# Feed-forward products of a hybrid decoder step on 2x2 blocks, with seven multiplications in place of eight

## Chip, cores and metric

The kernel runs on one core of one Trainium2 chip. The time is device microseconds of one execution, given as the median of several; a profiled execution has a time of its own, and its trace covers the span from the first to the last instruction. The engines are TensorE (PE, with its weight loads as PEld), VectorE (DVE), ScalarE (ACT), GpSimd (POOL) and SyncE (SP), which issues nearly all DMAs.

## What is computed

One layer of a decoder over 1024 prompt rows and 8 sample rows (1032 columns here, as tokens lie along the free dimension), all float32: a mixer (chunked gating and an RWKV-7 recurrence), cross-attention, a feed-forward part, and a final norm.

```python
def sq_relu_ffn(h, w_up, w_down):
    return jnp.square(jax.nn.relu(h @ w_up)) @ w_down
...
        x = x + y_mix
        x = x + cross_attn(rmsnorm(x, norm_x_g[l]), mem_k, mem_v, w_xq[l], w_xo[l])
        x = x + sq_relu_ffn(rmsnorm(x, norm_ffn_g[l]), w_up[l], w_down[l])
...
    y_prompt = rmsnorm(xp, final_g)
```

w_up is 1024 x 4096, w_down 4096 x 1024.

## The kernel before

Products keep float32 accuracy by splitting each operand into a high part that the PE takes (fp32r) and a low part, the rest. `gemm` (L132) runs three products for each 128 rows of the sum: high x high, high x low, low x high. `split` makes the parts: ACT casts (L99), DVE or POOL subtracts (L100).

Phase 1 is the mixer, in a hand-written order (`ORDER`). Phase 2 goes on in SBUF: the output projection w_out (`residual` splits each new row block of x into `x2`), the attention by heads, the projection w_xo (L1089, L1090: x is put together again from its two parts and added to), and `ffn`. A scheduler places the instructions of each engine by a model of their times, so program order and engine order differ a little; engines take their own instructions in order.

`ffn` goes through 8 groups of 512 hidden rows. For each of 4 tiles of 128 hidden rows it loads w_up columns (POOL scales them by the norm's weights, L115; ACT and DVE split), runs 3 blocks of 260, 260 and 512 tokens with 24 products each, and turns the result into the split square of its positive part (ACT L1281, L1282; POOL L1283; DVE L1284). Then the group's part of w_down: 8 tiles of 128 output rows, 3 blocks each, 12 products, added to `acc` by DVE (L1295). The hidden rows never leave SBUF. In the last group the blocks are finished in turn, and `last_norm` normalises and stores a tile while the next block's products run:

```python
            for (b0, b1), tiles in zip((*self.BLOCKS[0:2], (520, 776), (776, 1032)), ((0, 1), (2, 3, 8), (4, 5), (6, 7))):
                for m in range(KT):
                    down(ws[m], m, b0, b1)
                self.last_norm(tiles[0:2], acc, r2, gfin, f1, f2, pf)
```

Of the kernel before, what the change touches and what calls it, by code (L numbers as in the profile page):

```python
# [68 lines left out]
class K:  # L69
    ORDER = order()  # L70

    def __init__(self, ctx, tc, a, o, phases=9, dbg=None):
# [952 lines left out]
    def phase2(self, phases):  # L1025
        nc, tc, a = self.nc, self.tc, self.a
        N0 = HALF + NB

        def pool(cx, name, bufs, **k):
            return cx.enter_context(tc.tile_pool(name=name, bufs=bufs, reuse_waits="tile", **k))  # L1030
        with ExitStack() as c2:

            self.o0, self.x0, x1 = (pool(c2, nm, 1) for nm in ("o0", "x0", "x1"))
# [4 lines left out]
            self.ssacc = self.x0.tile([P, T], F32, name="ssacc")  # L1038
            self.x2 = [half(self.x0, "x20", 0), half(x1, "x21", 1)]
            with ExitStack() as c3:  # L1040
                o1 = pool(c3, "o1", 1)
                o = [half(self.o0, "o0", 0), half(o1, "o1", 1)]
                with ExitStack() as c4:
                    self.t2 = pool(c4, "t2", 2)
                    t2b = pool(c4, "t2b", 4)
                    for i, (h0, h1) in enumerate(((0, N0), (N0, T))):
                        oh, ol = o[i]
                        for k in range(0, KT, 2):
                            st = (t2b if i else self.t2).tile([P, 2, HALF], F32, tag="ost", name="ost")
                            nc.sync.dma_start(st, self.d_o[i][k:k + 2].rearrange("k p t -> p k t"))  # L1050
                            self.split(oh[:, k:k + 2, 0:HALF], ol[:, k:k + 2, 0:HALF], st)
                        if i == 0:
                            st = self.t2.tile([P, KT, NB], F32, tag="oss", name="oss", bufs=1)
                            nc.sync.dma_start(st, self.d_os.rearrange("k p t -> p k t"))
                            self.split(oh[:, :, HALF:], ol[:, :, HALF:], st)
                    for i, blocks in enumerate((((0, N0 // 2), (N0 // 2, N0)), ((N0, T),))):
                        for m in range(KT):
                            w = self.load_w(a["w_out"][0][:, m * P:(m + 1) * P])
                            n = N0 if i == 0 else HALF
                            xt = self.t2.tile([P, N0], F32, tag="xnew", name="xn")[:, 0:n]  # L1060
                            nc.sync.dma_start(xt, self.d_x[m][:, i * N0:i * N0 + n])
                            for b0, b1 in blocks:
                                ps = self.pg.tile([P, 512], F32, tag="g", name="ps_g")[:, 0:b1 - b0]
                                self.gemm(ps, w, *o[i], slice(b0 - i * N0, b1 - i * N0))
                                x = xt[:, b0 - i * N0:b1 - i * N0]
                                nc.vector.tensor_tensor(x, ps, x, op=ALU.add)  # L1066
                                self.residual(m, x, b0, b1, m == 0)
                self.ah = [half(self.o0, "o0", 0), half(o1, "o1", 1)]
                with ExitStack() as c4:
                    self.q1, self.q2 = pool(c4, "q1", 1), pool(c4, "q2", 2)  # L1070
                    self.pa = pool(c4, "pa", 2, space=PSUM)
                    self.sp = self.q1.tile([P, 2, NB, NB], F32, name="sp8")
                    nc.gpsimd.memset(self.sp, 0.0)
                    self.token_rs((0, 1, 2, 3, 8))
                    self.token_rs((4, 5, 6, 7))
                    for h in range(4):
                        self.attention(h, (1, 0, 2, 3))
                        if phases == 2:
                            return
                self.t2 = pool(c3, "t3", 2)  # L1080
                blocks = ((0, N0 // 2), (N0, T), (N0 // 2, N0))
                for ms in ((0, 1), (2,), (3,), (4,), (5,), (6,), (7,)):
                    ws = {m: self.load_w(a["w_xo"][0][:, m * P:(m + 1) * P]) for m in ms}
                    for m, (b0, b1) in [(m, b) for b in blocks for m in ms]:
                        ps = self.pg.tile([P, 512], F32, tag="g", name="ps_g")[:, 0:b1 - b0]
                        xh, xl, cols = self.halves(b0, b1)
                        self.gemm(ps, ws[m], *self.ah[0 if b0 < N0 else 1], cols)
                        x = self.t2.tile([P, N0], F32, tag="xnew", name="xn")[:, 0:b1 - b0]
                        nc.vector.tensor_tensor(x, ps, xh[:, m, cols].bitcast(F32), op=ALU.add)  # L1089
                        nc.vector.tensor_tensor(x, x, xl[:, m, cols].bitcast(F32), op=ALU.add)  # L1090
                        self.residual(m, x, b0, b1, m == 0)
            with ExitStack() as c5:
                self.ffn(pool(c5, "f1", 1), pool(c5, "f2", 2), pool(c5, "pf", 4, space=PSUM))
# [280 lines left out]
```

## Time and profile before

| | us |
|---|---|
| median of 3 runs | 1862.61 (1858.98 to 1871.34) |
| profiled execution, its time | 1867.79 |
| its span | 1866.1 |
| first feed-forward product | 1115.51 |
| last feed-forward product | 1854.90 |

Times in the views count from the start of the span. A row of the timeline gives start, length, engine, line, operation, output <- inputs, the tile's partitions x elements and how often; in brackets stands how long the engine had been idle and what ended that.

### The profile page before, as it was taken

What the parts mean: (1) busy time and instruction counts of PE and PEld (TensorE: products, weight loads), DVE (VectorE), ACT (ScalarE), POOL (GpSimd) and SP (SyncE); (2) the same over time, 40 slices, a digit from 0 to 9 for tenths busy, and PEclk for the clock granted to TensorE, in tenths of its full rate; (3) what the DMA queues carried; (4) which work ended last, traced back from release to release, by engine and by line L of the source; (5) the groups of instructions that cost most, each with busy time, mean ns of one, the idle gap of its engine ahead of it and who ended that gap; (6) DMA issues with size and microseconds to landing.
All of it is one profiled execution on the core that took longest, in us unless ns stands there. A gap on an engine that the chain in (4) does not pass through costs nothing.

```text
span 1866.1 us, 33959 instructions
## 1 busy us (share of the span) xinstructions
PE 1735.4 (93%) x13965; PEld 1545.9 (83%) x13965; DVE 1026.5 (55%) x2123; ACT 631.3 (34%) x1253; POOL 625.8 (34%) x530
## 2 busy tenths in 40 slices
PE   6998887998995699999999999999999999999998
PEld 6887777887884588878887898999998999999997
DVE  5697787679758846656565566324232323232335
ACT  4545443554432244433333332131312121212133
POOL 6551332134238563664333343121212121111210
PEclk8999887999896899999999999999999999999999
DMA  4413312111213483545443111112121202020212
GB/s 134 114 46 98 119 57 81 55 57 58 68 47 87 138 246 108 166 148 168 148 147 103 35 46 40 51 40 62 34 62 32 68 23 68 24 68 29 64 44 92
DMA packets 235884, 152.84 MB, mean 82 GB/s; under 512 B 20616, under 2 KB 219680, under 8 KB 235728
## 3 DMA queue, kind: packets, MB, share of 16 engines
q1 hardware_dynamic: 235684, 150.65, 27.1%
q8 instruction: 110, 1.80, 0.4%
q14 instruction: 46, 0.38, 0.1%
q10 hardware_dynamic: 44, 0.01, 0.0%
HBM read 131.07 MB, written 19.56 MB: 81 GB/s over the span
## 4 chain that ended last, share of the span: by engine, by line
PE 73%; DVE 13%; DMA 4%; issue 4%; ACT 3%; POOL 2%; SPq 0%; DVEq 0%; POOLq 0%; ACTq 0%
PE ps_g L132 59%; PE ps_kv L132 2%; PE ps_so L1232 2%; PE psgram L494 1%; DMA qb<-d_q 1%; DVE ptmp L555 1%; PE ps_o L1169 1%; PE psx L630 1%; POOL ck L1212 1%; DVE pb L556 1%; DVE st L466 1%; PE ps_sc L1155 1%; PE psz L638 1%; DVE sp L1187 1%; PE psf L616 1%
## 5 line engine op out<-in xcount | busy, mean ns | idle before, releaser
L132 PE MATMUL ps_g<-x,wh 128*128 128x260 f32 (+3 forms) x2048 | 445.3, 312 | 1.6 <-ACT rl L1281 1.6
L132 PEld LDWEIGHTS ps_g<-x,wh 128*128 128x128 f32 x2048 | 334.6, 189 | 28.0 <-ACT rl L1281 2.9
L132 PE MATMUL ps_g<-x,wl 128*128 128x260 f32 (+3 forms) x1024 | 317.2, 311 | 0.0
L132 PE MATMUL ps_g<-xh,wh 128*128 128x256 f32 (+1 forms) x704 | 217.6, 309 | 11.8 <-DVE raw L365 6.8
L99 ACT CAST wh<-wst 128x1024 fp32r<-128x1024 f32 x124 | 129.8, 1048 | 288.0 <-PE ps_g L132 208.9
L132 PE MATMUL ps_g<-xl,wh 128*128 128x256 f32 (+1 forms) x704 | 213.5, 303 | 1.1 <-DVE xl L100 1.1
L132 PE MATMUL ps_g<-xh,wl 128*128 128x256 f32 (+1 forms) x704 | 211.6, 301 | 0.1
L132 PE MATMUL ps_g<-sl,wdh 128*128 128x260 f32 (+1 forms) x672 | 211.5, 320 | 0.0
L132 PE MATMUL ps_g<-sh,wdh 128*128 128x260 f32 (+1 forms) x672 | 211.4, 320 | 0.0
L1295 DVE TENSOR_TENSOR acc<-ps_g,acc 128x260 f32<-128x260 f32 (+1 forms) x200 | 98.8, 500 | 198.9 <-PE ps_g L132 198.9
L100 POOL TENSOR_TENSOR wl<-wst,wh 128x1024 fp32r<-128x1024 f32 x70 | 171.0, 2443 | 107.8 <-ACT wh L99 92.1
L132 PE MATMUL ps_g<-sh,wdl 128*128 128x260 f32 (+1 forms) x672 | 204.5, 320 | 0.0
L132 PEld LDWEIGHTS ps_g<-x,wl 128*128 128x128 f32 x1024 | 192.6, 189 | 11.8
L115 POOL TENSOR_TENSOR wst<-wst,prm 128x1024 f32<-128x1024 f32 x40 | 76.0, 1901 | 329.6 <-DVE wdl L100 163.9
L132 PE MATMUL ps_g<-o,wh 128*128 128x260 f32 (+1 forms) x768 | 177.1, 325 | 3.1 <-DVE xn L1066 1.9
L1283 POOL TENSOR_TENSOR rl<-rl 128x260 f32<-128x260 f32 (+1 forms) x96 | 76.2, 795 | 247.6 <-ACT sh L1282 247.5
L132 PEld LDWEIGHTS ps_g<-xh,wh 128*128 128x128 f32 x704 | 143.6, 204 | 18.1 <-DVE raw L365 7.3
L132 PEld LDWEIGHTS ps_g<-xl,wh 128*128 128x128 f32 x704 | 143.3, 204 | 6.6 <-issue 2.4
L132 PEld LDWEIGHTS ps_g<-xh,wl 128*128 128x128 f32 x704 | 143.1, 203 | 3.8 <-issue 1.4
L132 PEld LDWEIGHTS ps_g<-o,wh 128*128 128x128 f32 x768 | 128.9, 191 | 16.5 <-issue 3.2
L1284 DVE TENSOR_TENSOR sl<-rl,sh 128x260 fp32r<-128x260 f32 (+1 forms) x96 | 50.1, 525 | 154.3 <-POOL rl L1283 154.3
L132 PEld LDWEIGHTS ps_g<-sh,wdh 128*128 128x128 f32 x672 | 126.0, 188 | 10.2
(444 smaller groups left out, 3392.1 us busy)
## 6 DMA issues: line engine op xcount, KB each, us to landing
wst<-in_w_in_dram SPq DMA_DIRECT2D x44, 512.0 KB
wst<-in_w_up_dram SPq DMA_DIRECT2D x32, 512.0 KB
wdst<-in_w_down_dram SPq DMA_DIRECT2D x64, 256.0 KB
wst<-in_w_out_dram SPq DMA_DIRECT2D x16, 512.0 KB
ck<-in_cache_mem_k_dram SPq DMA_DIRECT2D x32, 256.0 KB
ck<-in_cache_mem_v_dram SPq DMA_DIRECT2D x32, 256.0 KB
sbv<-d_sv SPq DMA_DIRECT2D x40, 128.0 KB
xt<-in_x_prompt_dram SPq DMA_DIRECT2D x8, 512.0 KB
```

The source lines that it names most:

```text
L99: (heng or nc.scalar.copy)(hi, src)
L100: (eng or nc.vector).tensor_tensor(lo, src, hi.bitcast(F32), op=ALU.subtract)
L115: nc.gpsimd.tensor_tensor(st, st, g.unsqueeze(2).broadcast_to([P, KT, P]), op=ALU.mult)
L132: nc.tensor.matmul(ps, l[:, k, :], r[:, cols], start=(k == 0 and i == 0), stop=(k == kt - 1 and i == 2))
L466: nc.vector.scalar_tensor_tensor(st[hr, :, h, 0:64], cs3(kkn[hr, :]), -1.0, lam[hr, :, 0:C], op0=ALU.mult, op1=ALU.mult)
L494: nc.tensor.matmul(psgs[h][:, ci, :], bk[hr, c].rearrange("p j t -> p (j t)"), st[hr, c, h, :], start=True, stop=True)
L555: nc.vector.tensor_tensor(tv, blocks[:, :, t + 1:16, t:t + 1].broadcast_to(shape), blocks[:, :, t:t + 1, 0:t].broadcast_to(shape), op=ALU. ...
L556: nc.vector.tensor_tensor(dst, dst, tv, op=ALU.add)
L1232: nc.tensor.matmul(po, pt[:, t, b, :], vts[b // 2][:, b % 2, t, :], start=(n == 0), stop=(n == 15))
L1283: nc.gpsimd.tensor_tensor(r[:, 0:n], r[:, 0:n], r[:, 0:n], op=ALU.mult)
L1284: nc.vector.tensor_tensor(sl[:, 0, b0:b1], r[:, 0:n], sh[:, 0, b0:b1].bitcast(F32), op=ALU.subtract)
L1295: nc.vector.tensor_tensor(acc[:, m, b0:b1], ps, acc[:, m, b0:b1], op=ALU.add)
```

## The change

Both feed-forward products are done on 2x2 blocks with Winograd's form of Strassen's scheme: seven block products of combined operands, and sums of the results. The token axis is cut in two halves of 516 columns (`HT`), which are one side of the blocks, and pairs of 128-row tiles are the other. An operand in `self.b` holds the seven combinations of 256 rows of x or of hidden rows, in high and low parts; there are four of them at a time (`cb0`, `cb1`, and two in the tiles that held the attention output). 16 turns (`turn`) make 256 hidden rows each, 16 more add 1024 hidden rows to 256 output rows. A turn is 7 steps (`STEPS`) of 2 half-blocks (258 columns, `HS`) of 12 products.

Per turn the weights of the next one are loaded in two tiles of 512 KB and combined on POOL (L1153 of the new file, 4 times), their 7 combinations split by ACT and DVE (L102, L103). Results are added up in `up` or `down`: PSUM to SBUF by ACT (2 steps) or DVE (5 steps), SBUF sums by POOL and DVE. Finished hidden rows go to DRAM (`d_h`), 256 rows or 1.06 MB per turn; each down turn but the last loads such a pair into the one buffer `hr` and replaces an operand with its combinations (L1118 on POOL, 4 times; ACT and DVE split 7). The last up turn replaces all four operands. x is written to DRAM after w_out and after w_xo (`d_x`), and kept as one float32 tile (`yq`) in place of two parts. The final norm starts when all products are done. Two pools of phase 1 change places.

```diff
@@
-        self.sb, self.xp, self.sa, self.s1 = (c1.enter_context(tc.tile_pool(name=nm, bufs=1)) for nm in ("sb", "xp", "sa", "s1"))
+        self.sb, self.sa, self.xp, self.s1 = (c1.enter_context(tc.tile_pool(name=nm, bufs=1)) for nm in ("sb", "sa", "xp", "s1"))
@@
...
+                        nc.sync.dma_start(self.d_x[m][:, i * N0:i * N0 + n], xt)
...
+            c3.close()
+            cb, yq, self.wx, hr = (pool(c2, nm, n) for nm, n in (("cb", 1), ("yq", 1), ("wx", 2), ("hr", 1)))
+            self.ssacc = yq.tile([P, T], F32, name="ssx")
+            self.yq = [yq.tile([P, 2, T], F32, name=f"yq{i}") for i in range(4)]
+            self.hr = hr.tile([P, 2, T], F32, name="hr")
+            self.b = [self.operand(cb, f"cb{i}") for i in range(2)]
+            with ExitStack() as c4:
+                self.t2 = pool(c4, "t3", 2)
+                self.cross_out()
+            self.b += [self.operand(self.o0, "o0"), self.operand(o1, "o1")]
+            f1 = pool(c2, "f1", 1)
+            pq, pf = pool(c2, "pq", 2, space=PSUM), pool(c2, "pf", 2, space=PSUM)
+            self.ffn(f1, pq, pf)
+
+    STEPS = (("A11", 0), ("S1", 3), ("S2", 4), ("S4", 2), ("S3", 5), ("A12", 1), ("A22", 6))
+    def operand(self, pl, tag):
+        t = pl.tile([P, 2, 7, HT], F32R, tag=tag, name=f"c_{tag}")
+        return t[:, 0], t[:, 1]
+    def combine(self, b, x, *what):
+        nc = self.nc
+        b11, b12, b21, b22 = (x[:, j, h * HT:(h + 1) * HT] for j in range(2) for h in range(2))
+        for c in what:
+            if isinstance(c, str):
+                dst, p, q = {"T1": (b11, b12, b11), "T3": (b12, b22, b12), "T2": (b22, b22, b11), "T4": (b21, b21, b22)}[c]
+                nc.gpsimd.tensor_tensor(dst, p, q, op=ALU.subtract)
+                continue
+            src = {0: b11, 1: b21, 2: b22, 3: b11, 4: b22, 5: b12, 6: b21}[c]
+            self.split(b[0][:, c], b[1][:, c], src)
+    AHEAD = {0: (0, "T1"), 1: (3, "T3"), 3: (2, "T2", 4), 4: (5,), 5: (1, "T4"), 6: (6,)}
+    def features(self, i):
+        nc, x = self.nc, self.yq[i]
+        for j in range(2):
+            nc.vector.tensor_scalar(x[:, j], x[:, j], self.g["norm_ffn_g"][:, 2 * i + j:2 * i + j + 1], None, op0=ALU.mult)
+        self.combine(self.b[i], x, *(c for n in range(7) for c in self.AHEAD.get(n, ())))
+    def hidden(self, step, b, pair, x):
+        if step == 0:
+            self.nc.sync.dma_start(x, self.d_h[pair])
+        self.combine(b, x, *self.AHEAD.get(step, ()))
+    def weights(self, step, it):
+        nc = self.nc
+        W, R = self.w.setdefault(it, ({}, {}))
+        def split(n):
+            k = 7 * it + [x[0] for x in self.STEPS].index(n)
+            pl, tag = ((self.wp, "wh"), (self.wp, "wl"), (self.wx, "wx"))[k % 3]
+            t = pl.tile([P, 2, 4, P], F32R, tag=tag, name=f"w{n}")
+            W[n] = t[:, 0], t[:, 1]
+            self.split(t[:, 0], t[:, 1], R[n])
+        def comb(n, dst, x, y, op):
+            R[n] = R[dst] if dst else self.wx.tile([P, 4, P], F32, tag=n, name=f"r{n}", bufs=1)
+            nc.gpsimd.tensor_tensor(R[n], R[x], R[y], op=op)
+        if step == 0:
+            if it < 16:
+                rows, cols, src = (0, 4), it, self.a["w_up"][0]
+            else:
+                rows, cols, src = (it - 16, it - 12), it % 4, self.a["w_down"][0]
+            src = src.rearrange("(i k p) m -> p i k m", k=2, p=P)[:, :, :, cols * 256:(cols + 1) * 256]
+            for r in range(2):
+                t = self.wp.tile([P, 4, 256], F32, tag="wst", name=f"wr{r}")
+                for q0, q1 in ((rows[0], min(rows[1], 16)), (16, rows[1])):
+                    if q0 < q1:
+                        nc.sync.dma_start(t[:, q0 - rows[0]:q1 - rows[0]], src[:, q0 % 16:q0 % 16 + q1 - q0, r])
+                R[f"A1{r + 1}"], R[f"A2{r + 1}"] = t[:, :, 0:P], t[:, :, P:256]
+        elif step == 1:
+            comb("S3", None, "A11", "A21", ALU.subtract)
+            comb("S1", "A21", "A21", "A22", ALU.add)
+            comb("S2", None, "A22", "S3", ALU.subtract)
+        elif step == 2:
+            split("A11")
+        elif step == 3:
+            split("S1")
+        elif step == 4:
+            split("S2")
+            comb("S4", "S2", "A12", "S2", ALU.subtract)
+        elif step == 5:
+            split("S4")
+        elif step == 6:
+            split("S3")
+            split("A12")
+            split("A22")
+    def turn(self, it, bs, banks, evict, ahead):
+        nc = self.nc
+        for n, (wn, c) in enumerate(self.STEPS):
+            hi, lo = self.w[it][0][wn]
+            for s in range(2):
+                pl, tag = banks[n % 4]
+                ps = pl.tile([P, 512], F32, tag=tag, name=f"ps_{wn}")[:, 0:HS]
+                cols = slice(s * HS, (s + 1) * HS)
+                for k, (i, b) in enumerate(bs):
+                    for j, (l, r) in enumerate(((hi, b[0]), (hi, b[1]), (lo, b[0]))):
+                        nc.tensor.matmul(ps, l[:, i, :], r[:, c, cols], start=k == 0 and j == 0, stop=k == 3 and j == 2)
+                evict(wn, s, ps)
+            ahead(n)
...
+            for m in ms:
+                nc.sync.dma_start(self.yq[m // 2][:, m % 2], self.d_x[m])
+            for m, (b0, b1) in [(m, b) for b in blocks for m in ms]:
+                ps = self.pg.tile([P, 512], F32, tag="g", name="ps_g")[:, 0:b1 - b0]
+                i = 0 if b0 < N0 else 1
+                self.gemm(ps, ws[m], *self.ah[i], slice(b0 - i * N0, b1 - i * N0))
+                x = self.yq[m // 2][:, m % 2, b0:b1]
...
+            if ms[-1] in (1, 3):
+                self.features(ms[-1] // 2)
+    def ffn(self, f1, pq, pf):
...
+        for step in range(7):
+            self.weights(step, 0)
+        for i in (2, 3):
+            self.features(i)
...
+        def up(n, s, ps):
+            y = yq[it % 4]
+            (c11, c12, c21, c22), whole = blocks(y, slice(s * HS, (s + 1) * HS), slice(0, HT))
+            if n in ("A11", "S1"):
+                nc.scalar.copy({"A11": c11, "S1": c22}[n], ps)
+            else:
+                dst, x = {"S2": (c21, c11), "S4": (c12, c12), "S3": (c21, c21), "A12": (c11, c11), "A22": (c21, c21)}[n]
+                nc.vector.tensor_tensor(dst, ps, x, op=ALU.add)
+            if s == 0:
+                return
+            w11, w12, w21, w22 = whole
+            if n == "S2":
+                nc.gpsimd.tensor_tensor(w12, w21, w22, op=ALU.add)
+            if n == "S3":
+                nc.gpsimd.tensor_tensor(w22, w22, w21, op=ALU.add)
+            for z in {"S4": (w12,), "S3": (w22,), "A12": (w11,), "A22": (w21,)}.get(n, ()):
+                nc.scalar.activation(z, z, AF.Relu)
+            if n in ("A12", "A22"):
+                z = y[:, int(n == "A22")]
+                nc.gpsimd.tensor_tensor(z, z, z, op=ALU.mult)
+                nc.vector.tensor_tensor(z, z, self.ssacc, op=ALU.mult)
+                nc.sync.dma_start(self.d_h[it][:, int(n == "A22")], z)
+        def down(n, s, ps):
+            y = yq[it % 4]
+            sc = slice(s * HS, (s + 1) * HS)
+            (c11, c12, c21, c22), (w11, w12, w21, w22) = blocks(y, sc, slice(0, HT))
+            if n == "S1" and s == 0:
+                self.s5 = f1.tile([P, HT], F32, tag="s5", name="s5")
+            s5 = self.s5
+            if n in ("A11", "S1"):
+                nc.scalar.copy((s1 if n == "A11" else s5)[:, sc], ps)
+            else:
+                c = {"S2": s1[:, sc], "S4": c12, "S3": s1[:, sc], "A12": c11, "A22": c21}[n]
+                nc.vector.tensor_tensor(c, ps, c, op=ALU.add)
+            if s == 1:
+                for eng, c, x in {"A11": (("p", w11, s1),), "S1": (("v", w12, s5), ("p", w22, s5)), "S2": (("p", w12, s1),),
+                                  "S3": (("v", w21, s1), ("p", w22, s1))}.get(n, ()):
+                    (nc.vector if eng == "v" else nc.gpsimd).tensor_tensor(c, c, x, op=ALU.add)
+        for it in range(32):
+            t = it - 16
+            if it < 16:
+                bs, new = list(enumerate(self.b)), ()
+                if it == 15:
+                    new = [(b, i, (yq[0], self.hr, yq[1], yq[2])[i]) for i, b in enumerate(self.b)]
+            else:
+                bs = [(i, self.b[(t + i) % 4]) for i in range(4)]
+                new = [(self.b[t % 4], (t + 4) % 16, self.hr)] if t < 15 else ()
+            def ahead(n):
+                if it < 31:
+                    self.weights(n, it + 1)
+                for b in new:
+                    self.hidden(n, *b)
+                if n == 6 and -1 <= t <= 2:
+                    nc.sync.dma_start(yq[t + 1], self.d_x[2 * t + 2:2 * t + 4].rearrange("k p t -> p k t"))
+            self.turn(it, bs, banks, up if it < 16 else down, ahead)
...
+                        nc.scalar.activation(q, x, AF.Square)
+                        (nc.vector if t == 15 else nc.gpsimd).tensor_tensor(cs, cs, q, op=ALU.add)
+        ps = token_sums("ps_rf")
...
```

Engine order, POOL, in the middle of the down products. Before, an eight-group repeats the following; `rl` is the positive part, `wst` the weights of w_up.

```order
L1283 TENSOR_TENSOR rl<-rl 128x260 x2
L1283 TENSOR_TENSOR rl<-rl 128x512
L115 TENSOR_TENSOR wst<-wst,prm 128x1024 x3
L1283 TENSOR_TENSOR rl<-rl 128x260
L115 TENSOR_TENSOR wst<-wst,prm 128x1024
```

Now, one down turn; `rS` and `wr` are combined and raw weights of the next turn, `hr` hidden rows, `yq` the output rows, `s1` and `s5` partial results.

```order
L1153 TENSOR_TENSOR rS3_17645<-wr0_17606 128x512
L1299 TENSOR_TENSOR yq0_11743<-yq0_11743,s1_12660 128x516
L1299 TENSOR_TENSOR yq0_11743<-yq0_11743,s5_17627 128x516
L1153 TENSOR_TENSOR wr0_17606<-wr0_17606,wr1_17608 128x4x128
L1153 TENSOR_TENSOR rS2_17648<-wr1_17608,rS3_17645 128x512
L1118 TENSOR_TENSOR hr_11747<-hr_11747 128x516
L1299 TENSOR_TENSOR yq0_11743<-yq0_11743,s1_12660 128x516
L1118 TENSOR_TENSOR hr_11747<-hr_11747 128x516
L1153 TENSOR_TENSOR rS2_17648<-wr1_17608,rS2_17648 128x512
L1118 TENSOR_TENSOR hr_11747<-hr_11747 128x516
```

Two of the three rows of L1153 that need `wr1`, the second weight tile, stand ahead of the first `hr` row. A `yq` and an `hr` row follow and end the turn's twelve.

DVE at the same place. Before (`acc` takes PSUM, `wdl` and `wl` are low parts of weights):

```order
L1295 TENSOR_TENSOR acc<-ps_g,acc 128x260 x3
L1295 TENSOR_TENSOR acc<-ps_g,acc 128x512
L100 TENSOR_TENSOR wdl<-wdst,wdh 128x512
L1295 TENSOR_TENSOR acc<-ps_g,acc 128x260
L1295 TENSOR_TENSOR acc<-ps_g,acc 128x512
```

Now, the second half of a turn (`c_cb0` is the operand that is replaced):

```order
L1299 TENSOR_TENSOR yq0_11743<-yq0_11743,s1_12660 128x516
L1295 TENSOR_TENSOR yq0_11743<-ps_A12_17757,yq0_11743 128x258
L103 TENSOR_TENSOR c_cb0_11748<-hr_11747,c_cb0_11748 128x516 x2
L1295 TENSOR_TENSOR yq0_11743<-ps_A12_17771,yq0_11743 128x258
L103 TENSOR_TENSOR wS4_17785<-rS2_17648,wS4_17785 128x512
L103 TENSOR_TENSOR wS3_17819<-rS3_17645,wS3_17819 128x512
L103 TENSOR_TENSOR c_cb0_11748<-hr_11747,c_cb0_11748 128x516
L1295 TENSOR_TENSOR yq0_11743<-ps_A22_17791,yq0_11743 128x258
L1295 TENSOR_TENSOR yq0_11743<-ps_A22_17805,yq0_11743 128x258
L103 TENSOR_TENSOR wA12_17822<-wr1_17608,wA12_17822 128x512
L103 TENSOR_TENSOR c_cb0_11748<-hr_11747,c_cb0_11748 128x516
```

Between the additions of results now stand subtractions and additions on SBUF tiles alone, in a fixed succession.

PE where the attention's output projection ends. Before, the first w_up products follow at once (`o` is the attention output, `x` the two parts of x):

```order
L132 MATMUL ps_g<-o_9344,wh 128x260 x2
L132 MATMUL ps_g<-o_9344,wl 128x260
L1099 MATMUL ps_rx<-ones,ssacc 128x1 x2
L1261 MATMUL ps_r_12574<-ssacc,ones 128x260
L132 MATMUL ps_g<-x_8427,wh 128x260 x2
```

Now the steps of the first turn are cut up, the two early operands first (`c_cb`), the two in the old tiles (`c_o`) later:

```order
L1239 MATMUL ps_r_12630<-ones,ssx 128x1 x2
L1195 MATMUL ps_A_12661<-c_cb_11748,wA_12568 128x258 x3
L1195 MATMUL ps_A_12661<-c_cb_11749,wA_12568 128x258 x3
L1195 MATMUL ps_S_12693<-c_cb_11748,wS_12571 128x258 x3
L1195 MATMUL ps_S_12693<-c_cb_11749,wS_12571 128x258 x3
...
L1195 MATMUL ps_S_12740<-c_cb_11748,wS_12574 128x258
L1195 MATMUL ps_A_12661<-c_o_12548,wA_12568 128x258
```

Nine half products' worth of the early operands stands ahead of or between the first of the late ones. Ahead of the feed-forward, SP's order gains one store to `d_x` after each w_out tile, and the loads of `yq` ahead of the w_xo products; else phase 1 and the attention keep their order.

## Rows read from the trace of the kernel before

**Rows 1.** The page: busy time by engine, PE in 40 slices, chain by engine.
```profile
PE 1735.4 (93%) x13965; PEld 1545.9 (83%) x13965; DVE 1026.5 (55%) x2123; ACT 631.3 (34%) x1253; POOL 625.8 (34%) x530
...
PE   6998887998995699999999999999999999999998
...
PE 73%; DVE 13%; DMA 4%; issue 4%; ACT 3%; POOL 2%; SPq 0%; DVEq 0%; POOLq 0%; ACTq 0%
```
**Rows 2.** Busy time by stage: us, busy us and instructions by engine, PEclk, DMA share, GB/s.
```profile
1300.00:1400.00 100.00, 100.00 (x643) 90.77 (x642) 32.34 (x54) 23.07 (x40) 19.57 (x19) 1.00 0.18 51
...
1855.00:1866.10 11.10, 1.93 (x18) 1.69 (x16) 3.95 (x10) 3.31 (x9) 0.00 (x0) 0.77 0.25 94
```
**Rows 3.** Timeline of PE: w_xo's last blocks, then the first feed-forward products.
```profile
1100.60 0.40 PE L132 MATMUL ps_g<-o,wh 128*128 128x260 f32 x2
...
1106.35 0.62 PE L132 MATMUL ps_g<-o,wh 128*128 128x512 f32 x2
...
1109.14 0.63 PE L132 MATMUL ps_g<-o,wh 128*128 128x512 f32 x2
...
1115.51 0.59 PE L132 MATMUL ps_g<-x,wh 128*128 128x260 f32 x2
...
1131.82 0.64 PE L132 MATMUL ps_g<-x,wh 128*128 128x260 f32 x2
...
1133.12 0.64 PE L132 MATMUL ps_g<-x,wh 128*128 128x260 f32 x2
```
**Rows 4.** Timeline of DVE and POOL in w_out, blocks of 260.
```profile
776.04 2.48 POOL L100 TENSOR_TENSOR wl<-wst,wh 128x1024 fp32r<-128x1024 f32 x1
776.21 0.42 DVE L1066 TENSOR_TENSOR xn<-ps_g,xn 128x260 f32<-128x260 f32 x1
...
777.10 1.70 DVE L100 TENSOR_TENSOR x<-xn,x 128x260 fp32r<-128x260 f32 x1 [0.47 <-ACT x L99]
778.48 0.93 POOL L1023 TENSOR_TENSOR ssacc<-ssacc,xsq 128x260 f32<-128x260 f32 x1
```
**Rows 5.** The same, a block of 512.
```profile
794.51 2.41 POOL L100 TENSOR_TENSOR wl<-wst,wh 128x1024 fp32r<-128x1024 f32 x1 [3.68 <-ACT wh L99]
...
794.99 2.48 DVE L100 TENSOR_TENSOR x<-xn,x 128x512 fp32r<-128x512 f32 x1 [0.72 <-ACT x L99]
796.88 1.74 POOL L1023 TENSOR_TENSOR ssacc<-ssacc,xsq 128x512 f32<-128x512 f32 x1
```
**Rows 6.** Groups by shape, 1100 to 1866: busy us, mean ns, idle before.
```profile
L1295 DVE TENSOR_TENSOR acc<-ps_g,acc 128x260 f32<-128x260 f32 x128 | 54.1, 426 | 80.7 <-PE ps_g L132 80.7
L1283 POOL TENSOR_TENSOR rl<-rl 128x260 f32<-128x260 f32 x64 | 41.9, 655 | 80.7 <-ACT sh L1282 80.5
...
L100 DVE TENSOR_TENSOR wdl<-wdst,wdh 128x512 fp32r<-128x512 f32 x56 | 38.3, 684 | 56.2 <-ACT wdh L99 56.2
L99 ACT CAST wdh<-wdst 128x512 fp32r<-128x512 f32 x56 | 34.8, 621 | 267.0 <-PE ps_g L132 267.0
L1283 POOL TENSOR_TENSOR rl<-rl 128x512 f32<-128x512 f32 x32 | 34.4, 1075 | 167.0 <-ACT sh L1282 167.0
...
L1340 DVE SCALAR_TENSOR_TENSOR fy<-ps_y,frs,gfin 128x512 f32<-128x512 f32 x16 | 10.9, 744 | 0.2
L1289 DVE TENSOR_TENSOR acc<-acc,ssacc 128x1032 f32<-128x1032 f32 x8 | 10.5, 1379 | 0.0
...
L1330 ACT ACT_TABLE_LOAD x1 | 1.3, 1283 | 0.0
```
**Rows 7.** Timeline: a weight load's issue, and the POOL operation that waited for it.
```profile
1306.75 0.37 SPq L107 DMA_DIRECT2D wst<-in_w_up_dram  x1
...
1311.12 1.90 POOL L115 TENSOR_TENSOR wst<-wst,prm 128x1024 f32<-128x1024 f32 x1 [1.88 <-DMA wst<-in_w_up_dram]
```
**Rows 8.** Timeline: the last product, and the last tiles' scaling.
```profile
1854.90 0.28 PE L132 MATMUL ps_g<-sh,wd 128*128 128x256 f32 x1
...
1860.24 2.73 DVE L1340 SCALAR_TENSOR_TENSOR fy<-ps_y,frs,gfin 128x512 f32<-128x512 f32 x4
```

More of the change, by code (lines that the diff above doesn't have):

```diff
@@ L26 @@
 T = SEQ + NB
+HT = T // 2
+HS = T // 4
 C = 64
@@ L1037, in half @@
                 return t[:, 0], t[:, 1]
[L1038 to L1091, printed above, removed]
@@ L1092, in phase2 @@
-            with ExitStack() as c5:
-                self.ffn(pool(c5, "f1", 1), pool(c5, "f2", 2), pool(c5, "pf", 4, space=PSUM))
+            self.ssacc = x0.tile([P, T], F32, name="ssacc")
+            self.x2 = [half(x0, "x20", 0), half(x1, "x21", 1)]
+            o = [half(self.o0, "o0", 0), half(o1, "o1", 1)]
+            with ExitStack() as c4:
+                self.t2 = pool(c4, "t2", 2)
+                t2b = pool(c4, "t2b", 4)
+                for i, (h0, h1) in enumerate(((0, N0), (N0, T))):
+                    oh, ol = o[i]
+                    for k in range(0, KT, 2):
+                        st = (t2b if i else self.t2).tile([P, 2, HALF], F32, tag="ost", name="ost")
+                        nc.sync.dma_start(st, self.d_o[i][k:k + 2].rearrange("k p t -> p k t"))
+                        self.split(oh[:, k:k + 2, 0:HALF], ol[:, k:k + 2, 0:HALF], st)
+                    if i == 0:
+                        st = self.t2.tile([P, KT, NB], F32, tag="oss", name="oss", bufs=1)
+                        nc.sync.dma_start(st, self.d_os.rearrange("k p t -> p k t"))
+                        self.split(oh[:, :, HALF:], ol[:, :, HALF:], st)
+                for i, blocks in enumerate((((0, N0 // 2), (N0 // 2, N0)), ((N0, T),))):
+                    for m in range(KT):
+                        w = self.load_w(a["w_out"][0][:, m * P:(m + 1) * P])
+                        n = N0 if i == 0 else HALF
+                        xt = self.t2.tile([P, N0], F32, tag="xnew", name="xn")[:, 0:n]
+                        nc.sync.dma_start(xt, self.d_x[m][:, i * N0:i * N0 + n])
+                        for b0, b1 in blocks:
+                            ps = self.pg.tile([P, 512], F32, tag="g", name="ps_g")[:, 0:b1 - b0]
+                            self.gemm(ps, w, *o[i], slice(b0 - i * N0, b1 - i * N0))
+                            x = xt[:, b0 - i * N0:b1 - i * N0]
+                            nc.vector.tensor_tensor(x, ps, x, op=ALU.add)
+                            self.residual(m, x, b0, b1, m == 0)
+                        nc.sync.dma_start(self.d_x[m][:, i * N0:i * N0 + n], xt)
@@ new lines, in phase2 @@
+            self.ah = [half(self.o0, "o0", 0), half(o1, "o1", 1)]
+            with ExitStack() as c4:
+                self.q1, self.q2 = pool(c4, "q1", 1), pool(c4, "q2", 2)
+                self.pa = pool(c4, "pa", 2, space=PSUM)
+                self.sp = self.q1.tile([P, 2, NB, NB], F32, name="sp8")
+                nc.gpsimd.memset(self.sp, 0.0)
+                self.token_rs((0, 1, 2, 3, 8))
+                self.token_rs((4, 5, 6, 7))
+                for h in range(4):
+                    self.attention(h, (1, 0, 2, 3))
+                    if phases == 2:
+                        return
```

182 lines of the change are left out of this document (87 added, 95 removed).

## Prediction

> **What bounds the kernel now.** I read the page first. The matrix engine (PE) is busy 93% of the span and carries 73% of the chain that ended last [rows 1]; a busy PE is not a PE at its peak, so the next view was busy time by stage. In the feed-forward stretch PE is busy for all of 1300 to 1400 us at granted clock 1.00, while VectorE (DVE) and GpSimd (POOL) are busy 32 and 20 us of 100 [rows 2]. There PE alone sets the time. The timeline gives the true price of a product, the distance from start to start: from 1100.60 to 1106.35 there are 48 products of 260 columns, 0.1198 us each, and from 1106.35 to 1109.14 twelve of 512 columns, 0.2325 us each [rows 3]. The "mean ns" of a group is a latency and is of no use here. Before, the two feed-forward products are 3072 of the first kind and 1536 of the second: 368 + 357 = 725 us, of the 750.6 us from the first of them at 1115.51 [rows 3] to the end of the span at 1866.1 us.
>
> **What the change removes.** Now there are 32 turns of 7 x 2 x 12 = 168 products of 258 columns. At 0.1198 x 258/260 = 0.1189 us a turn costs PE 20.0 us, all turns 639 us: 86 us less. That is the paper gain. It holds only while the helpers of a turn fit under 20.0 us.
>
> **What it adds beside PE.** The helpers are sums and differences, and they meet at one place. In [rows 4] a POOL operation runs from 776.04 to 778.52. The DVE addition that reads PSUM, started at 776.21, takes its usual 0.42 us. The DVE subtraction with both inputs in SBUF, started at 777.10, takes 1.70 us and ends at 778.80, 0.28 us after POOL; the next POOL operation, begun at 778.48, takes its turn behind it. With 512 elements [rows 5]: DVE ends 0.55 us after POOL's end at 796.92, and POOL's following 512-element sum ends 1.15 us after DVE's. So a DVE operation on two SBUF inputs and a POOL operation exclude each other: about 0.55 us of common access for 512 elements on DVE, 1.15 to 1.2 on POOL (I take 1.17), whatever each looks like alone (0.69 on DVE [rows 6]). POOL's squares, both inputs one tensor, take 0.65 us for 260 and 1.08 for 512 elements [rows 6], so 1.9 for 1032, 1.85 of access; DVE's 1032-element product 1.38 us [rows 6], 1.08 of access. Evictions from PSUM (0.43 us each [rows 6]) stay outside.
>
> The Trainium skill, "GPSIMD Engine Reference", section "8. Key points", says that POOL shares its SBUF interfaces with VectorE and contends with instructions with two SBUF inputs; the trace agrees, and goes further, since one waits for the whole of the other. If contention only slowed both a little, the down turn below would be hidden under 20.0 us: the first rival.
>
> *Up turn* (16 of them): access by DVE for 7 low parts of weights and 2 scalings, 3.9 + 2.2; by POOL for 4 weight combinations and 2 additions, 7.0, and 2 squares, 3.7. Sum 16.8 us, under 20.0: hidden, if little is lost in handing over. I take 20.0 us, up to 20.6.
>
> *Down turn* (16, the last without the helpers for a next one): DVE has 7 low parts of weights, 7 of hidden rows and 2 additions, 16 x 0.55 = 8.8; POOL 4 weight combinations, 4 of hidden rows and 4 additions, 12 x 1.17 = 14.0. Sum **22.8 us, above PE's 20.0**. The cover is gone: PE waits. Nor can the 22.8 be packed fully, since all hidden rows pass one buffer, hr. Its next load waits for the last split of the old pair; that is followed by 1.06 MB from DRAM. A 0.52 MB load issued at 1306.75 was used at 1311.12, 4.4 us later [rows 7]; for twice the bytes 4.4 to 8.8, taken 6.5. Then cast (0.62) and subtraction (0.69) of the first block. On POOL two weight combinations stand ahead of the first hidden one; they wait for the turn's second weight tile, which is issued right behind hr: at about 8 us, plus 2 x 1.17 = 10.4, first hidden combination done at 11.6. From there to the last split 12 DVE operations (0.55 to 0.69) and 6 POOL ones alternate, each needing the one before: 6.6 to 8.3 plus 7.0, middle 14.4. Together **26.0 us per turn**; 28.5 with the slow load, 22.8 as the floor. I take 26.0 because the queue order shown above has those operations in just this succession, and DVE holds evictions behind them. PE is ahead of DVE and waits on banks and split rows.
>
> **The joins.** *Start.* Two of four operands can be split only when the attention output projection has read the old contents of their tiles. 14 splits (7.7), 8 combinations (9.4), scaling of 4 rows (about 2.2, priced as splits, not seen before), sums of squares (1.2), weights of the next turn (4): 24.5 us of access, then two half products of 1.43: first turn 27 us (22 to 32). The 10 us of products on the two early operands fill only part. *Turn 15* replaces all four operands: up to the last split out of hr 28 DVE operations (15.4) and 22 POOL ones (14 + 4 + 2 of 1.17, 2 squares: 27) plus 1.8 until PE frees the first block: 44; seven splits and scalings left over, 5 more: 49 (40 to 56). *Squares for the last norm* put 11 POOL additions into the last three turns with helpers: 13, of which I count 10. *Last turn:* 3 us from the last split to the last product.
>
> *End.* Before, 11 us lie between the last product at 1854.90 and the end [rows 8], as tiles are normalised while products run. Now everything waits for the last product: eviction, square, addition 1.9; nine small products 1; table load 1.28 [rows 6], scalars 1.7; 12 evictions with scaling at 0.744 [rows 6] 8.9 (ACT and POOL do the other 6 beside them); last store 3.1, as from 1862.97 (the end of the row at 1860.24 [rows 8]) to the end of the span. Sum 18.
>
> *Ahead of the feed-forward.* Sixteen stores to d_x follow the w_out products on SP's queue, ahead of later weight loads, and the store must land before its one of two xn buffers is loaded again: 0.7 + at most 4.4 + 4.4 [rows 7] = 9.5 us, with the rows needed 8.6 us on (one projection of 48 x 0.12 = 5.7 and the first half of the next): 0 to 0.9 each, 0 to 14; I take 3. yq's loads and its stores before the first turn lie beside the 90 us of products of the attention output, as do the splits of the first two operands; in exchange DVE loses an addition and a split per block. Nothing either way (-2 to +4).
>
> **Sum from 1115.5:** 27 + 14 x 20.0 + 49 + 15 x 26.0 + 10 + 3 + 18 = 777, against 750.6: +26, with w_out +29 us. The profiled execution took 1867.79 us, so 1897 for it; the median of the three runs is 1862.61, 5 below it, so **1892 us**.
>
> **Rivals.** *PE stays the bound.* If DVE and POOL pass each other, or the access is held for less than these rows say, a down turn costs 20.0: 32 x 20.0 + 2 at the start + 6 in turn 15 (ACT has 28 casts of 0.62 there [rows 6] and 8 us besides) + 18 = 666: 85 us less, **1778**. For it: before, the stretch shows 32 and 20 us of 100 on the two [rows 2], so it seems free. Against: every meeting in [rows 4, 5] is a full wait. *Packed access.* The hr load and its queue hide fully and a turn costs 22.8 to 24: 15 x (26.0 - 23.4) = 39 less, **1853**, no change. For it: POOL has five operations not tied to hr to fill the load with. *The clock falls as well.* At 1131 us, after a short idle and one-column products, PE runs at the lower of its two levels and 260 columns take (1133.12 - 1131.82)/6 = 0.217 us [rows 3]. With 6 us of waiting in each down turn, half of its products at that price make 84 x 0.119 + 84 x 0.215 = 28 us, then PE is late for the chain: about 28.5 a turn, +37, **1929**. It decides once the waits come in one piece rather than between products. The Trainium skill, "TensorE: Matmul & The Clock Gate", section "HAM oscillation — how this bites in real kernels", describes waits in every step of a loop that slow the clock in each; the row at 1131 us agrees for one gap.
>
> **How the numbers follow.** A measurement of this kernel tells about 1% from no change: 1844 to 1881. Forecast (24.3 to 27.5 us a turn, 1866 to 1915) 0.50; packed 0.20; clock or a slower load 0.18; PE-bound 0.12. Forecast and clock are slower, but for the part of the forecast under 25.3 us a turn (0.10). Faster 0.14 (PE-bound and a little of packed), same 0.28, slower 0.58. The range takes in 22.8 and 28.5 us a turn with the bounds of the joins and leaves out PE-bound and the far end of the slow case: 1844 to 1938.
>
> **What would show it.** Up turns should repeat every 20 us with PE busy throughout; down turns every 26, with PE idle some 6 us in each, waiting for DVE or ACT; DVE's 516-element subtractions should average well over 0.69 us, about 1.2. The hr load should land 6 to 8 us after its issue, and DVE and POOL together fill the turn. The end should take 18 us after the last product. If DVE's mean on these stays near 0.7 and down turns repeat every 20 us, the step on exclusion is wrong and with it the forecast; if they exceed 28, the load of hr or the clock was undersized.

## The result and the profile after

The changed kernel takes 1953.91 us (median of 4 runs, 1952.16 to 1960.82), the kernel before 1863.09: a ratio of 1.0489 (95% interval 1.0445 to 1.0532), 91 us slower. The prediction was 1892, with a range up to 1938. The profiled execution took 1960.82 us, its span is 1959.1 us. The sign was right, the size was a third of what came.

Page and two stretches, in the columns of [rows 1, 2]:

```profile
PE 1711.7 (87%) x14667; PEld 1574.7 (80%) x14667; DVE 1415.2 (72%) x2412; ACT 755.1 (39%) x1501; POOL 1072.2 (55%) x766
...
PE   6989888989976899999999999999996688977887
...
DVE 12%; DMA 4%; issue 2%; PE 2%; POOL 1%; ACT 1%; POOLq 0%; DVEq 0%; SPq 0%; ACTq 0%
```
```profile
1300.00:1400.00 100.00, 94.41 (x772) 92.80 (x773) 71.21 (x88) 35.87 (x72) 61.44 (x37) 1.00 0.27 91
1700.00:1800.00 100.00, 80.37 (x623) 78.99 (x622) 79.82 (x90) 30.93 (x60) 67.06 (x44) 0.95 0.25 85
```

PE has all but left the chain. The 2% and the 73% before are not alike, as the chain of the changed kernel could be followed back only to 1501 us: from there on PE has 40 of its 455 us, where before it had 355 of 362. The up turns lie ahead of it, and are read from timelines and from run 1. VectorE and POOL, 32 and 20 busy us of 100 before, now have 71 and 61 in the up turns, and 80 and 67 in the down turns. From 1700 to 1800 PE does 623 products, so a down turn takes 168 x 100/623 = 27.0 us; from 1300 to 1400 it does 772, so an up turn takes 21.8 us by this count and not 20.0; between the first evictions of turns 2 and 14 lie 263.43 us, 21.95 a turn. The products themselves cost what was forecast: six of 258 columns start at 1370.30, the next six at 1371.01, 0.118 us each.

Groups by shape, 1100 to 1960, which answer to [rows 6]:

```profile
L103 DVE TENSOR_TENSOR wA<-wr,wA 128x512 fp32r<-128x512 f32 x96 | 138.0, 1439 | 0.0
...
L103 DVE TENSOR_TENSOR c_cb<-hr,c_cb 128x516 fp32r<-128x516 f32 x63 | 80.7, 1287 | 14.9 <-ACT c_cb L102 14.7
...
L1295 DVE TENSOR_TENSOR yq<-ps_A,yq 128x258 f32<-128x258 f32 x64 | 25.3, 413 | 1.5 <-PE ps_A L1195 1.5
```

The subtraction that took 0.684 us before takes 1.44 and 1.29 in these groups; the eviction out of PSUM is as before. That is the forecast of the exclusion step ("about 1.2").

**The up turn.** Timeline of SP, POOL, VectorE and PE over one turn (one kernel, four engines, in order of time):

```profile
1376.82 0.38 SPq L1164 DMA_DIRECT2D wr<-in_w_up_dram  x1
...
1381.58 1.29 POOL L1153 TENSOR_TENSOR wr<-wr,wr 128x512 f32<-128x512 f32 x1 [5.38 <-DMA wr<-in_w_up_dram]
...
1382.83 1.29 POOL L1153 TENSOR_TENSOR rS<-wr,rS 128x512 f32<-128x512 f32 x1
...
1384.09 1.75 POOL L1273 TENSOR_TENSOR yq<-yq 128x516 f32<-128x516 f32 x1
...
1385.87 0.76 DVE L1268 TENSOR_TENSOR yq<-ps_S,yq 128x258 f32<-128x258 f32 x2 [1.19 <-POOL yq L1273]
...
1387.71 0.95 PE L1195 MATMUL ps_A<-c_cb,wA 128*128 128x258 f32 x6 [1.44 <-DVE yq L1268]
...
1396.41 2.39 DVE L103 TENSOR_TENSOR wA<-wr,wA 128x512 fp32r<-128x512 f32 x1
...
1398.87 0.38 SPq L1164 DMA_DIRECT2D wr<-in_w_up_dram  x1
```

The second weight tile has one buffer, as `hr` has: the two tiles of a turn take both buffers that their pool has for them. Its load is issued at 1376.82 and lands 4.8 us later; POOL combines it; its last subtraction ends at 1398.80, and the next load leaves at 1398.87. That is a ring, a loop of waits through which the next load must wait for the last reader of the one before: 22.05 us. PE waits in it for an eviction that stands behind POOL's `yq` sum.

**The down turn**, the same way:

```profile
1757.72 0.34 SPq L1136 DMA_DIRECT2D hr<-d_h  x1
...
1759.43 8.71 SPq L1164 DMA_DIRECT2D wr<-in_w_down_dram  x2
...
1764.63 1.29 POOL L1153 TENSOR_TENSOR wr<-wr,wr 128x512 f32<-128x512 f32 x1 [5.78 <-DMA wr<-in_w_down_dram]
...
1767.14 1.76 POOL L1118 TENSOR_TENSOR hr<-hr 128x516 f32<-128x516 f32 x1
...
1773.96 1.63 PE L1195 MATMUL ps_A<-c_o,wA 128*128 128x258 f32 x6 [4.67 <-DVE s L1295]
...
1783.21 1.79 DVE L103 TENSOR_TENSOR c_cb<-hr,c_cb 128x516 fp32r<-128x516 f32 x1
...
1785.02 0.34 SPq L1136 DMA_DIRECT2D hr<-d_h  x1
```

First hidden combination done 11.2 us after the load's issue (forecast 11.6), from there to the last subtraction 16.1 (14.4): 27.3 us, and 27.0 on average over the 13 rings from 1544.58 to 1895.44 (26.0). PE stands for 4.67 us and goes on at the lower clock (granted 0.50 from 1774 to 1777; six products in 1.63 us, where it needs 0.88), and is not on the chain for it.

By the chain the load that counts here is not that of `hr`, but the second weight tile's. ScalarE takes up `hr` at 1762.85, while GpSimd stands until 1764.63 for the weight tile, which could be loaded only from 1759.43 on, when its own last split had ended. The cast on ScalarE, and the chain from one of these loads to the next (start, length, what):

```profile
1762.85 0.62 ACT L102 CAST c_cb<-hr 128x516 fp32r<-128x516 f32 x1 [7.53 <-DMA hr<-d_h]
```
```profile
1757.62 1.79 DVE wA L103
...
1759.43 5.07 DMA wr<-in_w_down_dram
...
1764.63 1.30 POOL wr L1153
...
1784.92 1.79 DVE wA L103
...
1786.72 5.72 DMA wr<-in_w_down_dram
```

So the weight tile's ring closes the down turn too: 27.3 us, beside `hr`'s ring of the same length. Of the 13 turns the chain passes through the weight tile's load in ten and through `hr`'s in three.

**The end**, beside [rows 8]:

```profile
1937.66 0.52 PE L1195 MATMUL ps_A<-c_o,wA 128*128 128x258 f32 x3
...
1949.48 6.97 SPq L1358 DMA_DIRECT2D out_dram<-fy  x10
```

From the last of these products at 1937.9 to the end of the span are 21 us, where 18 were forecast.

### The profile page after: what moved, and what is told of

It is laid out like the page before. It is cut to its first block, busy times and chain, and to the rows that moved or that the text cites. A ratio compares the mean times of both kernels' runs of the same rounds, so it can differ in the third digit from the quotient of the medians.

```text
span 1959.1 us, 36621 instructions
## 1 busy us (share of the span) xinstructions
PE 1711.7 (87%) x14667; PEld 1574.7 (80%) x14667; DVE 1415.2 (72%) x2412; ACT 755.1 (39%) x1501; POOL 1072.2 (55%) x766
## 5 line engine op out<-in xcount | busy, mean ns | idle before, releaser
L1195 PE MATMUL ps_S<-c_cb,wS 128*128 128x258 f32 x1536 | 233.0, 287 | 21.9 <-DVE yq L1268 8.5
L1195 PE MATMUL ps_S<-c_o,wS 128*128 128x258 f32 x1536 | 233.2, 286 | 17.0 <-DVE c_o L103 10.4
L1195 PE MATMUL ps_A<-c_cb,wA 128*128 128x258 f32 x1152 | 187.7, 301 | 54.1 <-DVE s L1295 34.7
L103 POOL TENSOR_TENSOR wl<-wst,wh 128x1024 fp32r<-128x1024 f32 x70 | 170.3, 2432 | 111.5 <-ACT wh L102 93.2
L135 PE MATMUL ps_g<-xh,wh 128*128 128x256 f32 (+1 forms) x704 | 219.0, 311 | 11.2 <-DVE raw L368 6.2
L1195 PEld LDWEIGHTS ps_S<-c_cb,wS 128*128 128x128 f32 x1536 | 206.2, 192 | 26.2 <-issue 11.4
L1195 PEld LDWEIGHTS ps_S<-c_o,wS 128*128 128x128 f32 x1536 | 206.1, 192 | 20.0 <-DVE c_o L103 11.2
L1195 PEld LDWEIGHTS ps_A<-c_cb,wA 128*128 128x128 f32 x1152 | 166.0, 206 | 58.7 <-ACT yq L1277 18.0
L1195 PE MATMUL ps_A<-c_o,wA 128*128 128x258 f32 x1152 | 185.7, 299 | 27.1 <-DVE s L1295 23.7
L1195 PEld LDWEIGHTS ps_A<-c_o,wA 128*128 128x128 f32 x1152 | 166.2, 206 | 28.4 <-ACT c_o L102 9.0
L102 ACT CAST wh<-wst 128x1024 fp32r<-128x1024 f32 x92 | 96.2, 1047 | 136.3 <-PE ps_g L135 78.4
L103 DVE TENSOR_TENSOR wA<-wr,wA 128x512 fp32r<-128x512 f32 x96 | 138.0, 1439 | 0.0
L135 PE MATMUL ps_g<-o,wl 128*128 128x260 f32 (+1 forms) x384 | 124.5, 325 | 1.4 <-POOL wl L103 1.4
L1153 POOL TENSOR_TENSOR wr<-wr,wr 128x512 f32<-128x512 f32 x32 | 43.4, 1356 | 143.8 <-DMA wr<-in_w_up_dram 77.7
L103 DVE TENSOR_TENSOR wS<-rS,wS 128x512 fp32r<-128x512 f32 x96 | 105.7, 1112 | 22.2 <-ACT wS L102 22.1
```

The costliest lines, as they stand in the source:

```text
L102: (heng or nc.scalar.copy)(hi, src)
L103: (eng or nc.vector).tensor_tensor(lo, src, hi.bitcast(F32), op=ALU.subtract)
L135: nc.tensor.matmul(ps, l[:, k, :], r[:, cols], start=(k == 0 and i == 0), stop=(k == kt - 1 and i == 2))
L1153: nc.gpsimd.tensor_tensor(R[n], R[x], R[y], op=op)
L1195: nc.tensor.matmul(ps, l[:, i, :], r[:, c, cols], start=k == 0 and j == 0, stop=k == 3 and j == 2)
```

## Experiments

The runs are compared by the interval between the first evictions of turns and by medians; ratios are to the kernel before, which had medians of 1864 to 1866 beside them.

**1. A second buffer for the weights of up turns.**

```diff
+                if it < 15 and it % 2:
+                    t = self.hr[:, r, 0:1024].rearrange("p (k c) -> p k c", k=4)
+                else:
                     t = self.wp.tile([P, 4, 256], F32, tag="wst", name=f"wr{r}")
```

> Raw weights of every other up turn go into the hidden-row buffer, which is idle until turn 15, so that a turn's second weight tile can be loaded while the last one's rows are still being split. Loop theory (an up turn repeats every 21.95 us because load, two combinations, additions and last splits of one weight tile follow each other in a ring): turns 1 to 14 at 20.0 to 20.6 us, 19 to 27 us less than the changed kernel's 1954, so 1927 to 1935, and the down turns as they were. Rival (handing over between VectorE and GpSimd costs the 2 us by itself, or GpSimd's order does): still 21.9 us a turn, 1950 to 1956.

Measured: 1933.83 us (ratio 1.0345, 1.0300 to 1.0391). Evictions of the first product (ACT), turns 2 and 14:

```profile
1173.48 0.38 ACT L1268 COPY yq<-ps_A 128x258 f32<-128x258 f32 x1 [0.28 <-PE ps_A L1198]
...
1414.63 0.38 ACT L1268 COPY yq<-ps_A 128x258 f32<-128x258 f32 x1 [0.27 <-PE ps_A L1198]
```

Twelve turns in 241.15 us, 20.1 each, against 21.95 in the changed kernel; down turns unchanged (27.3). The ring of the weight tiles made the 2 us: every operation and GpSimd's order are as they were, only the place of both tiles of every other turn is new.

**2. No sums on GpSimd.** All feed-forward sums go to VectorE, the squares to ScalarE; two of the seven edited lines:

```diff
-                nc.gpsimd.tensor_tensor(dst, p, q, op=ALU.subtract)
+                nc.vector.tensor_tensor(dst, p, q, op=ALU.subtract)
...
-                nc.gpsimd.tensor_tensor(z, z, z, op=ALU.mult)
+                nc.scalar.activation(z, z, AF.Square)
```

> All sums of the feed-forward that GpSimd did go to VectorE, the squares to ScalarE. Exclusion theory: with GpSimd silent, VectorE's operations on two SBUF tiles take their 0.69 us (0.605 from start to start); a down turn then has 28 x 0.605 + 10 x 0.335 = 20.3 us of VectorE, with the load's ring 21 to 23 us instead of 27; up turns near 20.0. About 1825 to 1865. Rival (these operations are slow for another reason, such as three tiles a partition apart, and VectorE is simply the busier engine): they stay at 1.2 us or more, a down turn takes over 30 us, and the kernel is slower than 2000.

Measured: **1815.8 us** (ratio 0.9731, 0.9690 to 0.9772), under the range expected and faster than both kernels. Groups and one stretch of the down turns:

```profile
L103 DVE TENSOR_TENSOR wA<-wr,wA 128x512 fp32r<-128x512 f32 x96 | 65.7, 684 | 17.2 <-ACT wA L102 17.0
...
L103 DVE TENSOR_TENSOR c_cb<-hr,c_cb 128x516 fp32r<-128x516 f32 x63 | 42.0, 688 | 0.0
```
```profile
1550.00:1650.00 100.00, 97.22 (x805) 96.39 (x804) 97.27 (x182) 42.92 (x85) 0.00 (x0) 1.00 0.29 96
```

VectorE does 12 operations more in a down turn and is done sooner: the same rows are back at 0.684 and 0.688 us. Down turns take 21.3, up turns 20.1 us, though the weight tile still has one buffer: PE alone is on the chain there, so the tile's ring is shorter than PE's turn now. PE and VectorE are both busy 97% in this stretch.

**3. No reload of hidden rows.**

```diff
+            if x is not self.hr or pair < 4:
-            self.nc.sync.dma_start(x, self.d_h[pair])
+                self.nc.sync.dma_start(x, self.d_h[pair])
```

> Left out: the loads of hidden rows in the down turns; their combinations are made of what the buffer holds. Ring theory (load, first weight combinations, alternating sums and splits, next load): the 5 us of the load, and the place of the second weight load behind it, leave the ring; a down turn falls from 27.0 to between 22.8, which the two engines' common access takes, and 24.5: 1905 to 1925. Rival (the load is hidden, the common access with its losses sets 27): 1948 to 1956.

Measured: 1921.58 us (ratio 1.0308, 1.0263 to 1.0354). Pairs 0 to 2, in the last turns, are still loaded; turns without a load come every 24.0 us. The longer pieces of the chain of waits, two turns; columns start, length, engine, tile, line:

```profile
1740.18 1.72 POOL hr L1118
1741.90 1.71 POOL yq L1300
1743.61 1.72 POOL wr L1154
1752.84 1.71 DVE yq L1300
1764.23 1.71 POOL hr L1118
1767.64 1.72 POOL wr L1154
1776.84 1.71 DVE yq L1300
```

Without `hr`'s load no DMA is left in this part of the chain: it goes through VectorE and POOL, but for one cast, and where both have work they take turns, 1.71 us a pair. 24.0 us is near the common access (22.8 by the prediction's sum). The 3 us less than 27.0 are not the load alone: as no load of `hr` stands ahead of them, the scheduler now puts a sum of `hr` and one of `yq` ahead of the first weight combination, into the time in which GpSimd stood for the weight tile. How much each gave is not shown. Turn 16 took 51 instead of 43 us here, between first evictions; why is not settled.

**4. Both.** The edits of 1 and 2.

> The first two together. If exclusion and the single weight tile are both real, up turns 20.0 and the rest as in the kernel without GpSimd's sums: equal to it if its up turns are already at 20.0, up to 25 us less if the weight tile's ring still shows there. 1820 to 1865. The rival of the second gives over 2000 here too.

Measured: 1810.92 us (0.9708, 0.9676 to 0.9739), 20.1 us an up turn, 21.4 a down turn: the gain of run 2 and, within the spread, no more, as its up turns were at PE's limit already.

**5. GpSimd busy beside, tied to nothing.** Into the kernel of run 2:

```diff
+            if t == 1:
+                p, q = self.ssacc[:, 0:HT], self.ssacc[:, HT:T]
+                for _ in range(40):
+                    nc.gpsimd.tensor_tensor(p, p, q, op=ALU.add)
...
+                    nc.gpsimd.tensor_tensor(p, p, p, op=ALU.subtract)
...
+                    nc.gpsimd.tensor_copy(p, q)
```

> The kernel without GpSimd's sums, and in its down turns 120 GpSimd operations of 516 elements on an idle tile that nothing waits for until turn 28: 40 additions of two different inputs, 40 subtractions with one tensor as both inputs, 40 copies. No dependency, queue or buffer of the products changes. Exclusion theory: beside the additions a VectorE operation on two SBUF tiles takes 1.7 us (its own 0.55 of access behind GpSimd's 1.17) and the stretch costs the turns about 40 x 1.17 = 47 us; evictions out of PSUM stay at 0.42; the subtractions cost about as much as GpSimd's squares, 40 x 1.0; of copies no row tells, 0 to 40 us. Together 1815 + 87 to 127. Rival (what cost time was GpSimd's slow links in the chain and its order, not the access): VectorE stays at 0.69 and the time at 1815 within 8.

Measured: 1895.7 us, 80 more than run 2, a little under the range of 1902 to 1942. Timeline of POOL and VectorE beside the additions:

```profile
1473.74 16.53 POOL L1319 TENSOR_TENSOR ssx<-ssx 128x516 f32<-128x516 f32 x10
...
1477.55 1.78 DVE L103 TENSOR_TENSOR wS<-rS,wS 128x512 fp32r<-128x512 f32 x1
1479.26 1.75 DVE L1153 TENSOR_TENSOR rS<-wr,rS 128x512 f32<-128x512 f32 x1
1480.94 1.76 DVE L1299 TENSOR_TENSOR yq<-yq,s 128x516 f32<-128x516 f32 x1
1482.62 1.76 DVE L1118 TENSOR_TENSOR hr<-hr 128x516 f32<-128x516 f32 x1
1484.31 0.75 DVE L1295 TENSOR_TENSOR yq<-ps_S,yq 128x258 f32<-128x258 f32 x2
```

One of each in turn, 1.69 us a pair; the two evictions between them take their usual 0.75 together. Beside the subtractions with one tensor a VectorE operation took 1.47 us, beside the copies about 1.0. Nothing of the products depends on these operations, so order and links are out: it is the access. The Trainium skill, "SBUF — State Buffer", section "Who interferes with whom", says that VectorE and GpSimd share a pair of ports as an exclusive lock, and that a VectorE instruction with two SBUF inputs contends with a GpSimd instruction that reads SBUF. These rows agree: one of each in turn, and the evictions, with one input in SBUF, at their usual length.

**6. and 8. Loads of hidden rows by single rows**, in the kernel of run 2, in all turns (6, whose edit is shown) and in down turns alone (8):

```diff
-            self.nc.sync.dma_start(x, self.d_h[pair])
+            for j in range(2):
+                self.nc.sync.dma_start(x[:, j], self.d_h[pair][:, j])
```

> The kernel without GpSimd's sums, its hidden rows loaded by two DMAs of one row each, so that the first can start when the combinations of that row are done. If the ring of load and combinations still sets its 21.3 us a down turn, they fall to 20.3 to 20.8, VectorE's own sum: 1800 to 1809. If VectorE's queue sets it (20.3 us of operations with gaps at evictions), no change: 1812 to 1820.

> As the kernel without GpSimd's sums, with two loads of one row only in the down turns (turn 15 loads its pairs whole again). If the earlier first row is worth what the last run showed (20.6 us a turn instead of 21.1) and the longer turns 15 and 16 there (63 us from turn 15 to 17 instead of 59) came from the divided loads of turn 15: 59 us there, 20.6 a down turn, 1803 to 1810. If the two are the scheduler's order and not the loads: about 1812 as in the last run.

Measured: 1811.74 (0.9725, 0.9683 to 0.9766) and 1818.57 us (0.9755, 0.9728 to 0.9781); down turns 20.9 and 21.3 us, turns 15 and 16 together 63 and 66 us where run 2 had 59. Both expectations of a gain missed. The middle turns of run 6 did fall, from 21.1 to 20.6 us, and the joins took it back; in run 8, where the same turns have the same loads, they are uneven (19.8 to 23.0). With 20.3 us of operations in VectorE's queue a turn, by the sum of run 2's expectation, an earlier load has little to give, and the order of the instructions moves as much.

**7. Only the hidden rows' sums on VectorE**, the first edit of run 2 alone.

> The changed kernel with only the four sums that combine hidden rows (and the rows of x) moved to VectorE. Common access of a down turn: VectorE 20 x 0.55 + GpSimd 8 x 1.17 = 20.4 us instead of 22.8, and the ring loses 4 x 0.6 us and what those sums waited for: 23 to 25 us instead of 27.3, up turns as in the changed kernel (21.95), attention's projection 3 to 6 us shorter: 1895 to 1920. Rival (the busier engine is the bound): VectorE gets 2.4 us more in each turn, 1954 or more.

Measured: 1913.89 us (1.0275, 1.0221 to 1.0328). Down turns 24 to 25 us, up turns 22.0; the stretch from the last w_out eviction to the last one of the attention's projection takes 285.5 us, against 291.8 in the changed kernel and 285.9 before. The time fits the expectation and not its rival.

## Why the prediction came out as it did

For the profiled execution the forecast was 1897, and 1960.8 came: 64 us more. Its terms, in its own order, turns by PE's products:

| term | forecast | measured | more |
|---|---|---|---|
| first feed-forward product | 1118.5 | 1118.3 | 0 |
| turn 0 | 27 | 31.5 | 4.5 |
| turns 1 to 14 | 280 | 304.1 | 24.1 |
| turn 15, to the next load of hr | 49 | 56.5 | 7.5 |
| turn 16, load to load | 26 | 34.1 | 8.1 |
| turns 17 to 29 (13 rings, 7 of the 10 us for squares) | 345 | 350.9 | 6 |
| last load of hr to the last product (26, 3 for squares, 3) | 32 | 42.5 | 10 |
| end | 18 | 21 | 3 |

**The step that failed** is "*Up turn*", with "16.8 us, under 20.0: hidden, if little is lost in handing over. I take 20.0 us, up to 20.6". The access was summed and held against PE's time, but the ring was not drawn: one buffer for the second weight tile, 4.8 us of load, combinations, eviction behind them, last subtraction. I drew just that ring for `hr` in the down turns and not for `wr1` here, though the two weight tiles of a turn take both buffers that their pool has for them, which leaves none for the next turn's. Run 1 shows that this, and not handing over, is the 2 us; with the ring opened the kernel takes 1933.83 us, inside the range. Turns 1 and 2 still took 20.1 and 20.5 us, so turns 1 to 14 lost 24 us and not 28.

**Right, by rows and runs:** the exclusion (run 5 by itself, run 2 by its removal), which evictions escape; the down turn as a ring through a load, 27.0 us against 26.0, or 26.5 with the squares; `hr`'s load, 5.1 us in the turn shown against 6.5; the access as a floor, 24.0 against 22.8 (run 3). Which load closes the ring was wrong in ten of the 13 turns: it is again the second weight tile's, which the forecast had only as standing behind `hr`'s. The number holds because both loads leave within 2 us of each other and the last splits of both tiles stand side by side. The clock did fall, but while VectorE and POOL set the end: the rival that priced it gave 28.5 us a turn. The rival of packed access (22.8 to 24 us) came true only with the load taken away. The PE-bound rival (20.0) is what run 2 nearly reaches once GpSimd is silent, as its condition has it.

**Sizes that were off:** the joins together 20 us (turns 0, 15 and 16: what turn 15 leaves over was counted as 5 us, and fills turn 16 as well), within the bounds given for turn 0 and just past those for turn 15. "*Last turn*: 3 us from the last split to the last product": PE was a turn behind and had most of its last 20 us still to do; the last subtraction of a hidden row ended at 1925.2, the last product at 1938. The *end* took 21 us: four sums of squares one after another, and stores that held the output buffers. *Ahead of the feed-forward* 3 us were put on the stores behind w_out. That stage took 106.1 us against 104.5, and 103.8 to 106.1 in the runs, which have the same stores: the 1.6 us are no more than it varies by. What came instead were 6 us in the attention's projection, where I took "nothing either way (-2 to +4)". GpSimd's sums of x there are the likely cause, not a shown one: with them that stage took 290.7 to 293.1 us (runs 1 and 3), without them 285.5 to 290.7 (the other six). The start of the feed-forward, 1118.3 us against 1118.5, agrees by luck: w_out began 4.3 us earlier than before. Where it begins differs by 10 us from run to run, with the same instructions ahead of it, so the change of pools can't be judged.

**Left open:** what turns 15 and 16 would take at best, turn 16 of run 3, and what a second buffer for the weights of the down turns would give.

## What to carry to other kernels

A tile that is loaded, combined and split, and has one buffer, is a ring: add up its load and everything up to its last reader, and hold that against the bound of the stage, for each such tile and not for the most obvious one. VectorE operations on two SBUF tiles and GpSimd's sums and copies are one resource: a sum moved to GpSimd to relieve VectorE cost 1.1 to 1.2 us of both, where VectorE alone did it in 0.605. Seven products for eight gained anything here, 50 us against the kernel before beside it, only after all sums had gone to one engine, and in the down turns VectorE is then as full as PE.

## What was not expected of the hardware

GpSimd's plain copies hold up VectorE too: beside them an operation on two SBUF tiles took about 1.0 us, not 0.69, beside operations with a single tensor as both inputs 1.47. While both had work, one of each ran in turn, so the cheaper engine was held to the pace of the pair.
